# Scan parameters of an S5 block: their rows turned behind the third tile of x, and their element-wise work written for GpSimd

## The chip, the cores and the metric

The kernel runs on one core of a Trainium2 chip. The metric is the device time of one execution in microseconds; three runs of the kernel before gave a median of 1979.87 us (1978.76 to 1980.63). The core has a matrix engine (TensorE, PE in the profile; its weight loads are PEld), VectorE (DVE), ScalarE (ACT), GpSimd (POOL) and SyncE (SP), which only issues transfers here. Each engine works through its own list of instructions in order, and waits at an instruction until the results it needs are there.

## The reference

The input x is 1024 tokens by 1024 channels in fp32, and the network is two blocks. The first block:

```
h    = rmsnorm(x, norm_mix_pre)
proj = h @ w_in                       # q 512, k 128, v 128, u 512, two gates of 1024
attn = sliding_window_attention(q, k, v, sinks, rel_bias)     # 8 heads of 64, window 128
ssm  = s5_ssm(u, lam_re, lam_im, log_dt, b_re, b_im, c_re, c_im, d_skip)
x    = x + gated merge of attn and ssm @ w_out;  then a squared-ReLU MLP of width 4096
```

The second block is a gated hybrid layer with a last rmsnorm. The scan, s5_ssm, has 32 groups of 16 channels with 64 complex states each, and its parameters are made from a few small tensors:

```
dt = exp(log_dt);  mag = exp(lr * dt);  ab = mag * (cos(li * dt) + i sin(li * dt))
f  = (ab - 1) / (lr + i li);            bb = f * b;     h_t = ab * h_(t-1) + bb u_t;     y = Re(c h)
```

So there are 16 x 128 values each of lam_re (lr) and lam_im (li), an exponential and a sine and cosine of each, and powers of ab, before the scan can be written as matrix products.

## The kernel before

**Products.** Every fp32 operand of a product is split in two fp16 parts: ScalarE writes the high part (line 136), VectorE the low one (line 137, scalar_tensor_tensor, STT), and TensorE makes three fp16 products of each pair (lines 214 to 216). Most projections go by a seven-product scheme (the function strassen): VectorE adds halves of the weights and of the activations beforehand (lines 166 to 172) and joins partial results (u at lines 237 and 243, c at 259) afterwards. The first two projections (first_pair, line 399, PSUM tiles called pq) use the plain eight by three products, since these can start with the first columns of x.

**The start.** x comes in eight tiles of 128 tokens. For each, ScalarE sums the squares (line 581), VectorE forms mean plus epsilon (line 442, the [128,1] tile rs), GpSimd raises it to the power -0.5 (line 444, in place), VectorE scales the tile (line 582), TensorE turns it with eight transposes (line 464, PSUM tiles tr), and ScalarE and VectorE split what comes out. GpSimd does little else: the power of each norm, and the issue of small transfers. VectorE then makes the sums for the seven-product scheme (sums_later), TensorE goes on with k, v and the first half of q.

**The scan's parameters** (lines 648 to 791 of the kernel before) are a unit of their own, in the program behind the second half of q, strassen(w_in, 256, ...). lam_re, lam_im and log_dt are loaded as rows of 16 x 128 (L16, in a piece of SBUF at 142 KB called arena), turned by three small transposes on TensorE (plp, line 658), and copied to the tile prm (line 661). From there VectorE works on tiles of 128 partitions with 16 values each (128x16), 32 or 128: EXP for dt (lines 664 to 679: a range reduction and a polynomial, where ki is a conversion to integers), EXP for the magnitudes (128x32), seven multiples of the angle (line 728, 128x16 each), SINCOS (lines 681 to 717, 128x128), the first power of ab (lines 732 and 733), powers by squaring (cmul, lines 637 to 646), the factors f_r and f_i (lines 741 to 753), and Bf = f * b by cmul on 128x256. The raw b (braw) lies in the same piece of SBUF as L16, so its two transfers, which GpSimd issues at line 756, wait for the three transposes. Attention comes next in the program, then u, then the scan.

**Order.** The Tile framework takes the program's units and sets a fixed order for each engine when it is built; the instructions of one engine then stay in that order. A unit written earlier gets its instructions earlier on every engine.

Of the kernel before, what the change touches and what calls it, by code (L numbers as in the profile page):

```python
# [15 lines left out]
ALU = mybir.AluOpType  # L16

P = 128
# [16 lines left out]
LN2_HI = 0.693145751953125  # L35
LN2_LO = 1.42860682030941723e-6
PIO2_1 = 1.5703125
PIO2_2 = float(np.floor((np.pi / 2 - 1.5703125) * 2.0**22) / 2.0**22)
PIO2_3 = float(np.pi / 2 - 1.5703125 - PIO2_2)
# [12 lines left out]
def kernel(ctx: ExitStack, tc: tile.TileContext, I: dict, out: bass.AP):  # L52
    nc = tc.nc
# [13 lines left out]
    def A32(kb, n):  # L67
        o = int(kb * KB) // 4
        return arena[:, o:o + n]

    def A16(kb, n):
        o = int(kb * KB) // 2
        return arena16[:, o:o + n]
# [19 lines left out]
    def nm(s):  # L93
        uid[0] += 1
        return f"{s}_{uid[0]}"

    def q2(name, n=H):
        t = pw.tile([P, H], F32, tag="q2", name=nm(name), bufs=NQ)
        return t if n == H else t[:, 0:n]
# [4 lines left out]
    def aux(name):  # L104
        return pps.tile([P, H], F32, tag="aux", name=nm(name), bufs=4)
# [17 lines left out]
    def small(shape, tag, bufs=1, dt=F32):  # L123
        return psm.tile(list(shape), dt, tag=tag, name=nm(tag), bufs=bufs)

    TS, STT, TT = nc.vector.tensor_scalar, nc.vector.scalar_tensor_tensor, nc.vector.tensor_tensor
# [3 lines left out]
    ident = small([P, P], "ident")  # L130
# [12 lines left out]
    def load_k(W, rows, c0):  # L143

        raw = pw.tile([P, 4, 256], F32, tag="raw", name=nm("raw"), bufs=NR)
        nc.sync.dma_start(out=raw, in_=rows(W)[:, :, c0:c0 + 256])
        return raw
# [287 lines left out]
    def rstd(ss, n, eps, serial=False):  # L435

        v = small([P, 1], "rs_1") if serial else small([P, 1], "rs_v", 3)
        if ss.shape[1] == 2:
            TT(v, ss[:, 0:1], ss[:, 1:2], ALU.add)
            TS(v, v, 1.0 / n, eps, ALU.mult, ALU.add)  # L440
        else:
            TS(v, ss, 1.0 / n, eps, ALU.mult, ALU.add)
        r = v if serial else small([P, 1], "rs_r", 3)
        nc.gpsimd.tensor_tensor(r, v, mhalf, ALU.pow)  # L444
        return r
# [85 lines left out]
    def halves(a):  # L531
        return [a[:, 0:H], a[:, H:2 * H]]
# [14 lines left out]
    def bias_rows():  # L547

        relb = small([33, 8], "relb")
        nc.vector.memset(relb, 1.0)  # L550
        nc.gpsimd.dma_start(out=relb[0:32, :], in_=I["rel_bias"])
        hot, row = A32(88, 384)[0:33, :], A32(89.5, 384)[0:8, :]
        nc.gpsimd.dma_start(out=hot, in_=I["onehot"])
        pb = aux("pbias")
        MM(pb[0:8, 0:384], relb, hot, start=True, stop=True)
        nc.scalar.copy(row, pb[0:8, 0:384])
        nc.gpsimd.dma_start(out=sink, in_=I["sinks"][0].partition_broadcast(P))
# [6 lines left out]
        skew = bass.AP(bdr.tensor, bdr.offset + 127, [[8 * 384 - 1, P], [384, 8], [1, 256]])  # L564
        nc.sync.dma_start(out=bias_t, in_=skew)

    kv_raws = []

    @do
    def _():  # L570
        xin = [A32((72, 56)[t // 4] + 4 * (t % 4), D) for t in range(NT)]
        for t in range(NT):
            nc.sync.dma_start(out=xin[t], in_=x[t * P:(t + 1) * P, :])
            if t == 0:
                nc.sync.dma_start(out=g_pre, in_=I["norm_mix_pre"][0].partition_broadcast(P))
            if t == 1:
                kv_raws.extend(load_k(w_in, HALVES[h], 512) for h in range(2))
        for t in range(NT):
            h, junk = xin[t], A16(134, D).bitcast(BF16)
            ss = small([P, 1], "ss1", 3)  # L580
            ACT(junk, xin[t], AF.Square, accum_out=ss)
            STT(h, xin[t], rstd(ss, D, 1e-6, True), g_pre, ALU.mult, ALU.mult)
            put_T(halves(h), t, hC, a21_1, lambda q, t: K32[q][:, :, (t % 4) * P:(t % 4 + 1) * P], later=True)
            if t == 1:
                prepare(1)
                bias_rows()


    q_t = A32(56, 4 * T).rearrange("p (c t) -> p c t", c=4)
# [34 lines left out]
    dsk = A32(140, G * C)[0:C, :].rearrange("p (r a c) -> p r a c", r=NP, a=2)  # L624
# [4 lines left out]
    def tmp(n, kb=None):  # L629
        if kb is not None:  # L630
            return A32(kb, n)
        a = A32(toff[0], n)
        toff[0] += n * 4 / KB
        assert toff[0] <= 134
        return a
# [11 lines left out]

    @do
    def _():
        L16 = tmp(3 * P, 142)[0:16, :].rearrange("p (i m) -> p i m", i=3)  # L650
        nc.gpsimd.dma_start(out=L16[:, 0, :], in_=I["lam_re"][0].rearrange("(r a) p -> r (a p)", a=2))
        nc.gpsimd.dma_start(out=L16[:, 1, :], in_=I["lam_im"][0].rearrange("(r a) p -> r (a p)", a=2))
        ldt = small([16, 2], "ldt")
        nc.gpsimd.dma_start(out=ldt, in_=I["log_dt"][0].rearrange("(r a) -> r a", a=2))
        nc.vector.tensor_copy(L16[:, 2, :].rearrange("p (a q) -> p a q", a=2), ldt.unsqueeze(2).to_broadcast([16, 2, 64]))
        plp = aux("plp")
        for i in range(3):
            nc.tensor.transpose(plp[:, i * 16:(i + 1) * 16], L16[:, i, :], ident[0:16, 0:16])
        keep = q2("prm")
        prm = keep[:, 0:48].rearrange("p (i r) -> p i r", i=3)  # L660
        nc.vector.tensor_copy(prm, plp[:, 0:48].rearrange("p (i r) -> p i r", i=3))
        lr, li = prm[:, 0, :], prm[:, 1, :]

        def EXP(dst, src, n):
            save, toff[0] = toff[0], 131.0
            xc, t, k, r, p = (tmp(n) for _ in range(5))
            ki = tmp(n).bitcast(I32)
            TS(xc, src, -87.0, 88.0, ALU.max, ALU.min)
            TS(t, xc, LOG2E, MAGIC, ALU.mult, ALU.add)
            TS(k, t, -MAGIC, None, ALU.add)  # L670
            STT(r, k, -LN2_HI, xc, ALU.mult, ALU.add)
            STT(r, k, -LN2_LO, r, ALU.mult, ALU.add)
            TS(p, r, 1.0 / 5040, None, ALU.mult)
            for c in (1.0 / 720, 1.0 / 120, 1.0 / 24, 1.0 / 6, 0.5, 1.0):
                STT(p, p, c, r, ALU.add, ALU.mult)
            TS(p, p, 1.0, None, ALU.add)
            TS(ki, k, 127.0, 8388608.0, ALU.add, ALU.mult)
            TT(dst, p, ki.bitcast(F32), ALU.mult)
            toff[0] = save

        def SINCOS(sn, cs, y, n):
            save, toff[0] = toff[0], 131.0
            t, q, r, r2, p, c = (tmp(n) for _ in range(6))
            s, o = r, r2
            TS(t, y, 2.0 / np.pi, MAGIC, ALU.mult, ALU.add)
            TS(q, t, -MAGIC, None, ALU.add)
            STT(r, q, -PIO2_1, y, ALU.mult, ALU.add)
            STT(r, q, -PIO2_2, r, ALU.mult, ALU.add)
            STT(r, q, -PIO2_3, r, ALU.mult, ALU.add)
            TT(r2, r, r, ALU.mult)  # L690
            TS(p, r2, 1.0 / 362880, None, ALU.mult)
            for cc in (-1.0 / 5040, 1.0 / 120, -1.0 / 6):
                STT(p, p, cc, r2, ALU.add, ALU.mult)
            STT(s, p, 1.0, r, ALU.add, ALU.mult)
            TS(p, r2, -1.0 / 3628800, None, ALU.mult)
            for cc in (1.0 / 40320, -1.0 / 720, 1.0 / 24, -0.5):
                STT(p, p, cc, r2, ALU.add, ALU.mult)
            TS(c, p, 1.0, None, ALU.add)

            TS(t, q, 0.5, -0.25, ALU.mult, ALU.add)  # L700
            TS(t, t, MAGIC, None, ALU.add)
            TS(t, t, -MAGIC, None, ALU.add)
            STT(o, t, -2.0, q, ALU.mult, ALU.add)
            TS(p, t, 0.5, -0.25, ALU.mult, ALU.add)
            TS(p, p, MAGIC, None, ALU.add)
            TS(p, p, -MAGIC, None, ALU.add)
            STT(p, p, -2.0, t, ALU.mult, ALU.add)
            TS(p, p, -2.0, 1.0, ALU.mult, ALU.add)
            TT(t, c, s, ALU.subtract)
            TT(t, t, o, ALU.mult)  # L710
            TT(t, t, s, ALU.add)
            TT(sn, t, p, ALU.mult)
            TT(t, c, s, ALU.add)
            TT(t, t, o, ALU.mult)
            TT(t, c, t, ALU.subtract)
            TT(cs, t, p, ALU.mult)
            toff[0] = save
# [44 lines left out]
        for i, n_ in enumerate(("c_re", "c_im")):  # L762
# [7 lines left out]
                nc.vector.tensor_copy(CT[a * 64:(a + 1) * 64, i], v[:, :, a, :])  # L770

        nc.gpsimd.dma_start(out=dsk.rearrange("p r a c -> p (r a c)"), in_=I["d_skip"][0].partition_broadcast(C))
        TT(dsk.rearrange("p r a c -> p (r a) c"), dsk.rearrange("p r a c -> p (r a) c"),
           ident[0:C, 0:C].unsqueeze(1).to_broadcast([C, G, C]), ALU.mult)

        for i, cs in enumerate((csd, snd)):
# [1 line left out]
        for k in range(4):  # L778
            m = 1 << k
# [430 lines left out]
    class InFacc:  # L1210
        a = [A16(128, 4 * 4 * H).rearrange("p (t h k c) -> p h t k c", t=4, h=4, k=4)[:, i] for i in range(2)]
# [348 lines left out]
```

## Time and profile before

| | us |
|---|---|
| median of three runs | 1979.87 |
| the profiled execution | 1979.92 |
| its span, first to last instruction | 1978.2 |
| TensorE busy | 1920.3 (97%) |
| VectorE busy | 1530.9 (77%) |
| ScalarE busy | 898.9 (45%) |
| GpSimd busy | 91.6 (5%) |

The profiled execution stands 0.05 us from the median, and 1.7 us of it lie outside the span. Busy times add up the durations of an engine's instructions; engines work beside each other, so the shares don't add up to one. Where TensorE is busy nearly all the time, an edit moves the end only so far as it opens or closes gaps in TensorE's row.

### The profile page before, as it was taken

Reading aid. Unit: us, or ns where it says so; the run is one execution under the profiler, and the core shown is the slowest. Engines: PE = TensorE matmul, PEld = TensorE weight load, DVE = VectorE, ACT = ScalarE, POOL = GpSimd, SP = SyncE. Lnnn points to the kernel's source line nnn. Section 1 sums busy time; section 2 is a strip of 40 time slices with the busy share of each in tenths; the row PEclk is TensorE's granted clock in tenths of the full one; section 3 lists DMA queues with packets and bytes.
Section 4 is the critical chain, followed back from the end, with each engine's and each line's share of the span. In section 5 each row is a group of like instructions: output and inputs, shape, how many; then the busy total and the mean of one; then the engine's idle time right before and its main releaser. Section 6 shows DMA issues by size and latency. Waiting matters only on the chain. (4 is left out here: it accounts for less than half of the span.)

```text
span 1978.2 us, 25744 instructions
## 1 busy us (share of the span) xinstructions
PE 1920.3 (97%) x9462; PEld 909.8 (46%) x9462; DVE 1530.9 (77%) x2817; ACT 898.9 (45%) x1702; POOL 91.6 (5%) x155
## 2 busy tenths in 40 slices
PE   7989998999999999999999999999999999999998
PEld 4445444444444444444454444454444444444443
DVE  7897878969579858868867667689688897899843
ACT  8437543344347536526546545435343343444411
POOL 1000101100010000000000011000000000000000
PEclk9999999999999999999999999999999999999999
DMA  7211633787221211211223422111211233333122
GB/s 237 69 59 44 134 97 90 222 273 232 65 96 43 64 56 51 64 61 47 65 75 108 118 92 78 43 44 54 74 54 54 64 86 75 86 75 96 49 80 85
DMA packets 133727, 176.01 MB, mean 89 GB/s; under 512 B 12353, under 2 KB 99653, under 8 KB 133472
## 3 DMA queue, kind: packets, MB, share of 16 engines
q1 hardware_dynamic: 126000, 163.09, 26.0%
q0 software_dynamic: 5424, 10.22, 3.5%
q8 instruction: 74, 1.21, 0.3%
q10 hardware_dynamic: 2176, 1.05, 0.2%
q14 instruction: 53, 0.43, 0.1%
HBM read 139.58 MB, written 30.95 MB: 86 GB/s over the span
## 5 line engine op out<-in xcount | busy, mean ns | idle before, releaser
L214 PE MATMUL b<-arena,whi 128*128 128x512 f16 x2044 | 776.8, 380 | 11.1 <-DVE u L243 3.1
L215 PE MATMUL b<-arena,whi 128*128 128x512 f16 x2044 | 776.6, 380 | 0.9 <-DVE arena L137 0.9
L216 PE MATMUL b<-arena,wlo 128*128 128x512 f16 x2044 | 776.6, 380 | 0.0
L136 ACT ACTIVATE whi<-raw 128x512 f16<-128x512 f32 x553 | 332.2, 620 | 504.6 <-PE b L215 237.2
L137 DVE SCALAR_TENSOR_TENSOR wlo<-raw,whi 128x512 f16<-128x512 f32 x553 | 369.6, 678 | 73.6 <-ACT whi L136 72.3
L215 PEld LDWEIGHTS <-whi 128*128 128x128 f16 x2044 | 200.4, 98 | 253.4 <-issue 19.3
L216 PEld LDWEIGHTS <-wlo 128*128 128x128 f16 x2044 | 200.4, 98 | 242.2 <-issue 6.2
L214 PEld LDWEIGHTS <-whi 128*128 128x128 f16 x2044 | 200.4, 98 | 240.4 <-issue 5.0
L259 DVE SCALAR_TENSOR_TENSOR c<-b,u 128x512 f32<-128x512 f32 x204 | 139.4, 684 | 53.6 <-PE b L216 53.4
L431 PEld LDWEIGHTS <-arena 128*128 128x128 f16 x1152 | 112.7, 98 | 133.2
L368 PE MATMUL pl<-arena,whi 128*128 128x512 f16 x320 | 82.4, 379 | 1.7 <-DVE fetch L1023 1.7
L431 PE MATMUL po<-arena 128*128 128x512 f16 x384 | 84.0, 379 | 0.0
L431 PE MATMUL pf<-arena 128*128 128x512 f16 x384 | 84.0, 379 | 0.0
L431 PE MATMUL pw<-arena 128*128 128x512 f16 x384 | 83.0, 379 | 0.0
L399 PE MATMUL pq<-arena,whi 128*128 128x512 f16 (+1 forms) x288 | 79.8, 361 | 0.1
L237 DVE SCALAR_TENSOR_TENSOR u<-b,p 128x512 f32<-128x512 f32 x79 | 54.2, 686 | 29.7 <-PE b L216 27.6
L243 DVE SCALAR_TENSOR_TENSOR u<-b,u 128x512 f32<-128x512 f32 x79 | 54.2, 686 | 29.4 <-PE b L216 29.3
L865 ACT ACTIVATE c<-c 128x512 f32<-128x512 f32 x60 | 37.7, 628 | 63.1 <-DVE c L259 58.0
L450 ACT ACTIVATE hn<-xr 128x512 f32<-128x512 f32 x32 | 19.9, 622 | 90.5 <-issue 40.1
L232 ACT ACTIVATE p<-b 128x512 f32<-128x512 f32 x79 | 46.1, 584 | 29.3 <-PE b L216 29.2
L136 ACT ACTIVATE arena<-c 128x512 f16<-128x512 f32 x67 | 41.8, 625 | 29.0 <-DVE c L1398 20.8
L444 POOL TENSOR_TENSOR rs_r<-rs_v,mhalf 128x1 f32<-128x1 f32 x48 | 27.6, 575 | 530.5 <-DVE rs_v L440 452.5
(326 smaller groups left out, 2066.8 us busy)
## 6 DMA issues: line engine op xcount, KB each, us to landing
raw<-in_w_in_dram SPq DMA_DIRECT2D x86, 512.0 KB, 4.0
raw<-in_w_ff_in_dram SPq DMA_DIRECT2D x32, 512.0 KB, 4.0
raw<-in_w_ff_out_dram SPq DMA_DIRECT2D x32, 512.0 KB, 4.2
fetch<-gdr SPq DMA_DIRECT2D x32, 256.0 KB, 5.2
xr<-xdr SPq DMA_DIRECT2D x32, 256.0 KB, 3.5
gdr<-c SPq DMA_DIRECT2D x24, 256.0 KB, 2.1
arena<-in_x_dram SPq DMA_DIRECT2D x8, 512.0 KB, 9.9
raw<-in_w_out_dram SPq DMA_DIRECT2D x8, 512.0 KB, 6.5
```

What stands on the lines that cost most here:

```text
L136: ACT(hi, src, AF.Copy, scale=scale)
L137: STT(lo, src, scale, hi, ALU.mult, ALU.subtract)
L214: MM(b[:, 0:n], whi[:, k], act[0][:, i, k, sl], start=(first and k == 0), stop=False, skip_group_check=not first)
L215: MM(b[:, 0:n], whi[:, k], act[1][:, i, k, sl], start=False, stop=False, skip_group_check=not first)
L216: MM(b[:, 0:n], wlo[:, k], act[0][:, i, k, sl], start=False, stop=(k == nk - 1), skip_group_check=not first)
L232: ACT(v["p1"], o1, AF.Copy, scale=scale)
L237: STT(v["u2"], o2, scale, v["p1"], ALU.mult, ALU.add)
L243: STT(v["u3"], o, scale, v["u2"], ALU.mult, ALU.add)
L259: STT(d, vw(o), scale, vw(v[u]), ALU.mult, ALU.add)
L368: MM(bs[s], w[:, k], a[:, k, s * H:(s + 1) * H], start=(k == 0 and w is hi and a is act[0]), stop=(k == 3 and w is lo))
L399: MM(o, w[:, k % 4], a, start=(k == 0 and w is hi and a is ahi), stop=(k == 7 and w is lo))
L431: MM(bs[s], part(a), w[:, s * H:(s + 1) * H], start=(k == 0 and a is ahi and w is whi), stop=(k == nk - 1 and a is alo))
```

## The change

The three loads of the parameters' rows, the three transposes and the copy to prm leave the parameters' unit for a function of their own, scan_rows, which is called in the loop over the tiles of x behind tile 2. In the unit itself the local names TS and TT become GpSimd's tensor_scalar and tensor_tensor, and STT, which GpSimd does here in two steps, becomes a helper that issues a TS and a TT through a temporary. On VectorE stay the conversions to integers (ki), the reciprocal, the two memsets, cmul, and the copies.

```diff
--- before.py
+++ after.py
@@ -564,7 +564,21 @@
         skew = bass.AP(bdr.tensor, bdr.offset + 127, [[8 * 384 - 1, P], [384, 8], [1, 256]])
         nc.sync.dma_start(out=bias_t, in_=skew)
 
-    kv_raws = []
+    kv_raws, scan_in = [], []
+
+    def scan_rows():
+
+        L16 = A32(142, 3 * P)[0:16, :].rearrange("p (i m) -> p i m", i=3)
+        for i, n_ in enumerate(("lam_re", "lam_im")):
+            nc.gpsimd.dma_start(out=L16[:, i, :], in_=I[n_][0].rearrange("(r a) p -> r (a p)", a=2))
+        ldt = small([16, 2], "ldt")
+        nc.gpsimd.dma_start(out=ldt, in_=I["log_dt"][0].rearrange("(r a) -> r a", a=2))
+        nc.vector.tensor_copy(L16[:, 2, :].rearrange("p (a q) -> p a q", a=2), ldt.unsqueeze(2).to_broadcast([16, 2, 64]))
+        plp = aux("plp")
+        for i in range(3):
+            nc.tensor.transpose(plp[:, i * 16:(i + 1) * 16], L16[:, i, :], ident[0:16, 0:16])
+        scan_in.append(q2("prm"))
+        nc.vector.tensor_copy(scan_in[0][:, 0:48], plp[:, 0:48])
 
     @do
     def _():
@@ -584,6 +598,8 @@
             if t == 1:
                 prepare(1)
                 bias_rows()
+            if t == 2:
+                scan_rows()
 
 
     q_t = A32(56, 4 * T).rearrange("p (c t) -> p c t", c=4)
@@ -647,18 +663,16 @@
 
     @do
     def _():
-        L16 = tmp(3 * P, 142)[0:16, :].rearrange("p (i m) -> p i m", i=3)
-        nc.gpsimd.dma_start(out=L16[:, 0, :], in_=I["lam_re"][0].rearrange("(r a) p -> r (a p)", a=2))
-        nc.gpsimd.dma_start(out=L16[:, 1, :], in_=I["lam_im"][0].rearrange("(r a) p -> r (a p)", a=2))
-        ldt = small([16, 2], "ldt")
-        nc.gpsimd.dma_start(out=ldt, in_=I["log_dt"][0].rearrange("(r a) -> r a", a=2))
-        nc.vector.tensor_copy(L16[:, 2, :].rearrange("p (a q) -> p a q", a=2), ldt.unsqueeze(2).to_broadcast([16, 2, 64]))
-        plp = aux("plp")
-        for i in range(3):
-            nc.tensor.transpose(plp[:, i * 16:(i + 1) * 16], L16[:, i, :], ident[0:16, 0:16])
-        keep = q2("prm")
+
+        TS, TT = nc.gpsimd.tensor_scalar, nc.gpsimd.tensor_tensor
+
+        def STT(out, in0, c, in1, op0, op1, t=None):
+            t = in0 if t is None else t
+            TS(t, in0, c, None, op0)
+            TT(out, t, in1, op1)
+
+        keep = scan_in[0]
         prm = keep[:, 0:48].rearrange("p (i r) -> p i r", i=3)
-        nc.vector.tensor_copy(prm, plp[:, 0:48].rearrange("p (i r) -> p i r", i=3))
         lr, li = prm[:, 0, :], prm[:, 1, :]
 
         def EXP(dst, src, n):
@@ -668,13 +682,13 @@
             TS(xc, src, -87.0, 88.0, ALU.max, ALU.min)
             TS(t, xc, LOG2E, MAGIC, ALU.mult, ALU.add)
             TS(k, t, -MAGIC, None, ALU.add)
-            STT(r, k, -LN2_HI, xc, ALU.mult, ALU.add)
-            STT(r, k, -LN2_LO, r, ALU.mult, ALU.add)
+            STT(r, k, -LN2_HI, xc, ALU.mult, ALU.add, t)
+            STT(r, k, -LN2_LO, r, ALU.mult, ALU.add, t)
             TS(p, r, 1.0 / 5040, None, ALU.mult)
             for c in (1.0 / 720, 1.0 / 120, 1.0 / 24, 1.0 / 6, 0.5, 1.0):
                 STT(p, p, c, r, ALU.add, ALU.mult)
             TS(p, p, 1.0, None, ALU.add)
-            TS(ki, k, 127.0, 8388608.0, ALU.add, ALU.mult)
+            nc.vector.tensor_scalar(ki, k, 127.0, 8388608.0, ALU.add, ALU.mult)
             TT(dst, p, ki.bitcast(F32), ALU.mult)
             toff[0] = save
 
@@ -684,9 +698,9 @@
             s, o = r, r2
             TS(t, y, 2.0 / np.pi, MAGIC, ALU.mult, ALU.add)
             TS(q, t, -MAGIC, None, ALU.add)
-            STT(r, q, -PIO2_1, y, ALU.mult, ALU.add)
-            STT(r, q, -PIO2_2, r, ALU.mult, ALU.add)
-            STT(r, q, -PIO2_3, r, ALU.mult, ALU.add)
+            STT(r, q, -PIO2_1, y, ALU.mult, ALU.add, t)
+            STT(r, q, -PIO2_2, r, ALU.mult, ALU.add, t)
+            STT(r, q, -PIO2_3, r, ALU.mult, ALU.add, t)
             TT(r2, r, r, ALU.mult)
             TS(p, r2, 1.0 / 362880, None, ALU.mult)
             for cc in (-1.0 / 5040, 1.0 / 120, -1.0 / 6):
@@ -700,7 +714,7 @@
             TS(t, q, 0.5, -0.25, ALU.mult, ALU.add)
             TS(t, t, MAGIC, None, ALU.add)
             TS(t, t, -MAGIC, None, ALU.add)
-            STT(o, t, -2.0, q, ALU.mult, ALU.add)
+            STT(o, t, -2.0, q, ALU.mult, ALU.add, p)
             TS(p, t, 0.5, -0.25, ALU.mult, ALU.add)
             TS(p, p, MAGIC, None, ALU.add)
             TS(p, p, -MAGIC, None, ALU.add)
@@ -770,7 +784,7 @@
                 nc.vector.tensor_copy(CT[a * 64:(a + 1) * 64, i], v[:, :, a, :])
 
         nc.gpsimd.dma_start(out=dsk.rearrange("p r a c -> p (r a c)"), in_=I["d_skip"][0].partition_broadcast(C))
-        TT(dsk.rearrange("p r a c -> p (r a) c"), dsk.rearrange("p r a c -> p (r a) c"),
+        nc.vector.tensor_tensor(dsk.rearrange("p r a c -> p (r a) c"), dsk.rearrange("p r a c -> p (r a) c"),
            ident[0:C, 0:C].unsqueeze(1).to_broadcast([C, G, C]), ALU.mult)
 
         for i, cs in enumerate((csd, snd)):
```

The two orders, engine by engine. First GpSimd's list from the pow of tile 3 of x on, before (arena is SBUF scratch, rs_34 the rs tile of tile 3, then 4, 5, 6 and 7; in_b_re_dram is the raw b):

```order
L444 TENSOR_TENSOR rs_34_194<-rs_34_194,mhalf_75 128x1
L444 TENSOR_TENSOR rs_38_216<-rs_38_216,mhalf_75 128x1
L444 TENSOR_TENSOR rs_42_238<-rs_42_238,mhalf_75 128x1
L444 TENSOR_TENSOR rs_46_260<-rs_46_260,mhalf_75 128x1
L444 TENSOR_TENSOR rs_50_282<-rs_50_282,mhalf_75 128x1
L756 DMA arena<-in_b_re_dram 128x16x16
L756 DMA arena<-in_b_im_dram 128x16x16
```

and from the same place after the change (rs_37 is tile 3, rs_41 tile 4; lines 671 to 684 are EXP, 756 to 758 the denominator of f):

```order
L444 TENSOR_TENSOR rs_37_205<-rs_37_205,mhalf_75 128x1
L770 DMA arena<-in_b_re_dram 128x16x16
L770 DMA arena<-in_b_im_dram 128x16x16
L682 TENSOR_SCALAR arena<-prm_201 128x16
L756 TENSOR_TENSOR prm_201<-prm_201 128x16
L757 TENSOR_TENSOR prm_201<-prm_201 128x16
L444 TENSOR_TENSOR rs_41_227<-rs_41_227,mhalf_75 128x1
L683 TENSOR_SCALAR arena<-arena 128x16
L758 TENSOR_TENSOR prm_201<-prm_201 128x16
L684 TENSOR_SCALAR arena<-arena 128x16
L671 TENSOR_SCALAR arena<-arena 128x16
L672 TENSOR_TENSOR arena<-arena 128x16
```

The two transfers of b now stand between the pows of tiles 3 and 4, with three element-wise instructions; 21 more stand between tiles 4 and 5, 31 between 5 and 6, nine (two on 128x32, seven on 128x128) between 6 and 7, and 44 behind tile 7. GpSimd's whole list grows from 143 rows to 252.

VectorE's list where it reads tiles 5 and 6 of x, before (rs_42 is tile 5, rs_46 tile 6; lines 442 and 582 are the mean and the scaling):

```order
L442 TENSOR_SCALAR rs_42_238<-ss_41_236 128x1
L582 SCALAR_TENSOR_TENSOR arena<-arena,rs_42_238 128x1024
L442 TENSOR_SCALAR rs_46_260<-ss_45_258 128x1
L137 SCALAR_TENSOR_TENSOR arena<-tr_220,arena 128x4x128
L137 SCALAR_TENSOR_TENSOR arena<-tr_225,arena 128x4x128
L582 SCALAR_TENSOR_TENSOR arena<-arena,rs_46_260 128x1024
```

and after (rs_45 is tile 5, rs_49 tile 6; line 596 is the scaling, 691 the conversion ki, 759 the reciprocal):

```order
L442 TENSOR_SCALAR rs_45_249<-ss_44_247 128x1
L691 TENSOR_SCALAR arena<-arena 128x16
L759 RECIPROCAL prm_201<-prm_201 128x16
L596 SCALAR_TENSOR_TENSOR arena<-arena,rs_45_249 128x1024
L691 TENSOR_SCALAR arena<-arena 128x32
L137 SCALAR_TENSOR_TENSOR arena<-tr_231,arena 128x4x128
L137 SCALAR_TENSOR_TENSOR arena<-tr_236,arena 128x4x128
L442 TENSOR_SCALAR rs_49_271<-ss_48_269 128x1
L596 SCALAR_TENSOR_TENSOR arena<-arena,rs_49_271 128x1024
```

Three instructions that read what GpSimd makes now stand between VectorE's work on the tiles of x. VectorE's list shrinks from 2722 rows to 2646; the block of cmul begins at its row 72, and u2 and u3 of the first seven-product projection stand at rows 119 and 129, where they stood at 78 and 80. On TensorE the three transposes plp stand behind six pq products that follow tile 2's transposes; the first logits of attention come 120 products of lines 214 to 216 earlier than before.

## Rows read from the trace of the kernel before

**Rows 1.** The page's head: span, and busy us of each engine.
```profile
span 1978.2 us, 25744 instructions
...
PE 1920.3 (97%) x9462; PEld 909.8 (46%) x9462; DVE 1530.9 (77%) x2817; ACT 898.9 (45%) x1702; POOL 91.6 (5%) x155
```

**Rows 2.** Windows: stretch, us, busy by engine (instructions), TensorE's clock, DMA, GB/s.
```profile
20.00:40.00 20.00, 19.38 (x149) 15.86 (x148) 16.40 (x27) 18.47 (x37) 2.74 (x5) 1.00 0.75 222
...
100.00:140.00 40.00, 33.74 (x147) 16.34 (x146) 37.20 (x166) 11.73 (x37) 1.50 (x2) 0.91 0.18 60
...
130.00:140.00 10.00, 7.35 (x23) 3.92 (x22) 8.78 (x39) 6.89 (x29) 0.00 (x0) 0.66 0.14 54
40.00:60.00 20.00, 20.00 (x94) 9.06 (x93) 20.00 (x18) 13.86 (x18) 0.00 (x0) 1.00 0.14 41
```

**Rows 3.** TensorE's waits, 100 to 140 us: total, times, longest.
```profile
PE b L214 <- DVE u L237: 1.8, 1, 1.8
...
PE b L214 <- DVE arena L706: 0.8, 1, 0.8
```

**Rows 4.** Timeline of GpSimd (POOL): start, us, instruction, idle before and releaser.
```profile
32.15 0.55 POOL L444 TENSOR_TENSOR rs<-rs,mhalf 128x1 f32<-128x1 f32 x1 [2.52 <-DVE rs L442]
...
88.81 1.23 POOL L756 DMA_DIRECT2D arena<-in_b_re_dram  x1 [56.12 <-PE plp L658]
93.62 1.18 POOL L756 DMA_DIRECT2D arena<-in_b_im_dram  x1 [3.58 <-issue]
```

**Rows 5.** Timeline of TensorE (PE), the same columns.
```profile
20.75 0.42 PE L399 MATMUL pq<-arena,whi 128*128 128x256 f16 x1
20.96 0.42 PE L399 MATMUL pq<-arena,wlo 128*128 128x256 f16 x1
...
35.30 1.26 PE L464 MATMUL tr<-ident,arena 128*128 128x128 f32 x8 [0.55 <-ACT arena L499]
...
70.00 0.38 PE L214 MATMUL b<-arena,whi 128*128 128x512 f16 x1
...
88.22 0.35 PE L658 MATMUL plp<-ident,arena 16*128 16x16 f32 x3
```

**Rows 6.** Timeline of VectorE (DVE) at tile 7 of x.
```profile
31.85 0.15 DVE L442 TENSOR_SCALAR rs<-ss 128x1 f32<-128x1 f32 x1 [0.53 <-ACT arena L136]
32.73 1.28 DVE L582 SCALAR_TENSOR_TENSOR arena<-arena,rs 128x1024 f32<-128x1024 f32 x1 [0.73 <-POOL rs L444]
```

**Rows 7.** Timeline of GpSimd, its first element-wise instructions.
```profile
0.31 0.10 POOL L1546 MEMSET const-float32-0.0<- 128x1 f32 x1 [0.31 <-issue]
...
2.26 0.33 POOL masks.py:199 TENSOR_SCALAR_AFFINE_SELECT ident<-ident 128x128 f32<-128x128 f32 x1
```

**Rows 8.** Timeline of GpSimd, tile 0's pow.
```profile
11.08 0.88 POOL L444 TENSOR_TENSOR rs<-rs,mhalf 128x1 f32<-128x1 f32 x1 [1.80 <-DVE rs L442]
```

**Rows 9.** Timeline of VectorE beside GpSimd's work.
```profile
10.84 1.50 DVE L137 SCALAR_TENSOR_TENSOR wlo<-raw,whi 128x512 f16<-128x512 f32 x2
...
93.96 0.17 DVE L726 TENSOR_TENSOR prm<-prm,dt 128x16 f32<-128x16 f32 x1
94.08 0.69 DVE L723 TENSOR_SCALAR prm<-prm 128x16 f32<-128x16 f32 x1
```

**Rows 10.** Groups of VectorE by shape, 88 to 140 us: busy, mean ns.
```profile
L697 DVE SCALAR_TENSOR_TENSOR arena<-arena 128x128 f32<-128x128 f32 x4 | 1.2, 289 | 0.1
...
L675 DVE SCALAR_TENSOR_TENSOR arena<-arena 128x16 f32<-128x16 f32 x6 | 1.0, 174 | 0.2
...
L639 DVE TENSOR_TENSOR arena<-prm,arena 128x256 f32<-128x256 f32 x1 | 0.4, 417 | 0.0
```

**Rows 11.** Timeline of VectorE at the first seven-product projection.
```profile
63.42 0.69 DVE L166 TENSOR_TENSOR raw<-raw,raw 128x512 f32<-128x512 f32 x1
...
75.45 0.69 DVE L237 SCALAR_TENSOR_TENSOR u<-b,p 128x512 f32<-128x512 f32 x1 [1.52 <-PE b L216]
...
77.97 0.69 DVE L243 SCALAR_TENSOR_TENSOR u<-b,u 128x512 f32<-128x512 f32 x1 [1.23 <-PE b L216]
```

## The prediction

> **What bounds the kernel now.** I read the page's head first: TensorE is busy 1920.3 of 1978.2 us [rows 1], so an edit moves the end only through the 57.9 us in which TensorE has nothing to do. Next the windows [rows 2]. From 20 to 40 us, where this change puts work, TensorE is busy 19.38 of 20 us: a delay there is a delay of the end, unless something later gives it back. From 100 to 140 us it is busy 33.74 of 40, so 6.26 us are idle, and its granted clock is 0.91 on the mean, down to 0.66 in the last ten microseconds (between the two levels, 1.2 and 2.4 GHz, some of both). VectorE is busy 37.20 of these 40 us, and the waits name it: 1.8 us for u, 0.8 us for a step of SINCOS [rows 3]. So there VectorE sets the pace, with the scan's parameters among its work, and that is what can be won.
>
> **Where the new work stands.** GpSimd now raises one number per row to a power for each tile of x, in 0.55 us [rows 4]; from this comes VectorE's scaling, then the turn on TensorE, in a list that is in order. After the change the two transfers of b and 64 element-wise instructions stand in GpSimd's list ahead of the pow of tile 7, and tiles 4 to 7 each wait for a part of them. TensorE's list has no other work to put there: the transposes of tiles 4 to 7 stand between the pq products, in order.
>
> First the time at which GpSimd can begin. The transfers of b wait for the transposes plp, which stand six pq products behind tile 2's. These products begin at 20.75 us, 0.21 us apart, and three small transposes take 0.35 us [rows 5]: 20.75 + 6 x 0.21 + 0.35 = 22.4, with the hand-over 22.55. In the trace of before the two issues run from 88.81 to 94.80, 5.99 us, of which 3.58 us are a gap ahead of the second that no other engine explains [rows 4]. That gives 28.5 us. If the gap doesn't recur, 2.41 us are left and it is 25.0; with DMA at 0.75 [rows 2] it can also be longer than in a quieter stretch, and I allow 3 us more. I take 28.5.
>
> Then the price of one dependent instruction on GpSimd, which the trace doesn't show for 16 elements. The hand-over: tile 7's mean ends at 32.00 on VectorE and its pow starts at 32.15 [rows 4, 6], so 0.15 us. Its own time is at least that of the smallest memset, 0.10 us, and a pow of one element takes 0.55 [rows 4, 7]. So p lies between 0.10 (no hand-over within the engine) and 0.55 us; I take 0.15 + 0.12 = 0.27, since a multiplication is nearer to the memset than a power is. For 128 columns the nearest row is the select on 128x128, 0.33 us [rows 7]; with the hand-over w = 0.48, bounds 0.2 and 0.8.
>
> Ahead of tile 7's pow: 50 dependent small instructions x 0.27 = 13.5; the seven independent multiples of the angle x 0.10 = 0.7; seven wide ones x 0.48 = 3.4; the pows of tiles 4 to 7, 4 x 0.55 = 2.2; VectorE's two conversions in between, there and back, 0.5. Sum 20.3, so tile 7's pow ends at 28.5 + 20.3 = 48.8 us. Before, it ended at 32.70 [rows 4]: 16.1 us later. Of this 1.3 us is slack: tile 7 was scaled at 34.01 [rows 6] and its transposes began at 35.30, waiting for ScalarE at the last [rows 5]. **The start loses 14.8 us**, bounds 0.8 (p 0.10, w 0.2, no gap: 34.8 us) and 31 (p 0.55, w 0.8: 65.0 us). VectorE's and ScalarE's work on the tiles shifts along with it.
>
> Two smaller terms. While TensorE waits from tile to tile its clock may fall, as in the stretch of 130 to 140 us, where idle time and a clock of 0.66 stand together and 3.4 us of clock are lost [rows 2]; between 0 and 3.4 I take 1. And GpSimd and VectorE slow each other: a pow took 0.88 us instead of 0.55 beside two low-part splits of VectorE [rows 8, 9], and a VectorE instruction on 16 columns 0.69 instead of 0.17 beside the issue of b_im [rows 4, 9]. Before tile 7 VectorE mostly waits itself; for the rest I take 2, bounds 0 and 14 (below).
>
> **What is removed and moved.** VectorE loses 34 instructions on 128 columns x 0.29 and some 44 small ones x 0.17 [rows 10], about 17 us, and the cmul that stays on it moves ahead of the stretch of 100 to 140 us. The idle time of that stretch, 6.26 us, and its clock, 40 x 0.09 = 3.6, are the most that can come back: 9.9 us. Not all of it will, since the wait for c_re's transfer and attention's own waits for VectorE stay. I take 6.5, bounds 0 and 9.9. Behind VectorE there, the next limit is TensorE itself. The order brings attention 120 products forward (26 us at 0.21); that moves work, and takes none away.
>
> Three edits I cost at nothing. The 44 instructions behind tile 7, 44 x 0.48 = 21, end near 70 us; VectorE reaches the cmul that needs them where line 166 began at 63.42 [rows 11], now at 78.2: 8 us of cover. The 44 rows of cmul ahead of u3, some 10 us at 0.17 to 0.42 [rows 10], fit in about: VectorE's old work in that stretch, 10.3 us, and these end at 63.4 + 20 = 83 by the old times, and TensorE, which makes a product group in 2.5 us [rows 11], needs u3 gone at 70.0 + 5 x 2.59 = 83 [rows 5]. With VectorE late, this cover is the first to go. And the copy and the three transposes cost the same at either place.
>
> **The sum.** 1979.92 + 14.8 + 1 + 2 - 6.5 = 1991 us. The profiled execution stands at the median of the runs (0.05 us off), so this is also the forecast for the median. Its own range, with p from 0.18 to 0.40 (tile 7's pow 4.5 us sooner or 6.5 later), is 1985 to 2000.
>
> **Rivals.**
> (B) GpSimd's small instructions are cheap, and the loss at the start falls under the gain. With p 0.10, w 0.33 and no gap before b_im, tile 7's pow ends at 25.0 + 5.0 + 0.7 + 2.3 + 2.2 + 0.5 = 35.7, the start loses 1.7, and with 6.5 to 9.9 back the time is 1972 to 1975, say 1974: faster. With the gap it loses 5.2, and 1979 is no change. It decides from a loss under 2.5 us on. For it: memsets of 0.10 us follow one another without a wait. Against it: the pow's 0.55 us for one element, a hand-over of 0.15 wherever an instruction waits for another, and the 3.58 us gap [rows 4, 6].
> The Trainium skill speaks for a price near B's: "GPSIMD Engine Reference", section 3.1, gives an add of two fp32 inputs with 2048 columns as 4497 ns at about 2.6 cycles per element. An estimate from that page is about 0.1 us for 16 columns and 0.34 for 128, without waits, and the sum by it would be B's with the gap. No row here shows GpSimd adding or multiplying, and its one-element pow of 0.55 us is well above that estimate.
> (C) The two engines shut each other out behind tile 7. From 40 to 60 us VectorE is busy 20.0 of 20 [rows 2], with work on SBUF; if each of the 44 instructions adds 0.33 us as the pow did [rows 8], GpSimd ends 14.5 us later, at 84, VectorE waits for it at the cmul or has lost as much itself, u2 and u3 come late, and TensorE waits up to that time: 1991 + 13 = 2004. For it: the two slowed instructions above; against it: one of them stood beside the issue of a transfer, not beside arithmetic.
> The Trainium skill states this as a rule: by "SBUF — State Buffer", section "SBUF: two separate sides", GpSimd and a VectorE instruction with two SBUF inputs take a shared port pair by turns, each for the whole instruction. The pow at 0.88 us agrees with that [rows 8, 9]; whether it also holds up VectorE on the path, no row shows.
> (D) GpSimd's arithmetic costs as much as its pow, p = 0.55: the start loses 31 us, and GpSimd ends at 65 + 44 x 0.8 = 100 where VectorE wants it at 94: 1979.9 + 31 + 1 + 2 - 6.5 + 3 = 2010.
> That the framework would hide the change doesn't arise: the order of each list is known.
>
> **How the numbers follow.** Forecast 0.45, B 0.25, C 0.15, D 0.15. This kernel's runs tell about 0.2%, 4 us, from no change, so faster is below 1976 and slower above 1984. Slower: 0.40 of the forecast's 0.45 (a cheap p with the full gain falls short of it), C and D, 0.70. No change: 0.05 of the forecast and 0.07 of B, 0.12. Faster: the rest of B, 0.18. The range reaches from the lower part of B to D, 1974 to 2010; what is left out are B with the full gain, and D with both engines in each other's way.
>
> **What would show it.** Right: the pows of tiles 4 to 7 at about 29, 36, 45 and 48 us, each behind an instruction of GpSimd's; tile 7's transposes near 50 us instead of 35.3; idle time of TensorE between 20 and 50 us named after VectorE's scaling, and VectorE's after GpSimd; no wait at the cmul; less than 2 us idle where 100 to 140 us stood before. Wrong in the first step: the second transfer of b issued at 24 us, or dependent instructions less than 0.2 us apart. Wrong in the cover: GpSimd's last product of SINCOS later than VectorE's line 166, and TensorE waiting for u. Wrong in the gain: the same idle time beside attention although VectorE has room.

## The result and the profile after

Slower: the median of four runs is 2001.12 us (1999.58 to 2003.55), beside 1980.11 for the kernel before; the ratio is 1.0107, 95% interval 1.0095 to 1.0119, so 21 us. The profiled execution took 2000.92 us with a span of 1999.2, which is 21.0 us more than in [rows 1]. (The row in [rows 8] is tile 1's pow, not tile 0's as its line says; nothing hangs on that. And GpSimd has 115 new element-wise instructions, 270 beside 155: 64 stand ahead of tile 7's pow, as was counted, and 51 behind it; the 44 of the count are those up to the product that cmul waits for.)

The page's head after the change, busy us by engine:

```profile
span 1999.2 us, 25776 instructions
...
PE 1925.1 (96%) x9462; PEld 913.1 (46%) x9462; DVE 1523.6 (76%) x2731; ACT 898.1 (45%) x1702; POOL 151.8 (8%) x270
```

TensorE's work is the same 9462 matmuls. Of the 21.0 us, 16.2 are time in which it has nothing to do (74.1 us beside 57.9) and 4.8 are longer busy time, for which the windows below show a lower clock. GpSimd's busy time went from 91.6 to 151.8 us, and VectorE's fell by only 7. The place of the loss is in the windows (stretch, us, busy by engine, TensorE's clock, DMA, GB/s):

```profile
20.00:40.00 20.00, 12.13 (x73) 9.40 (x72) 6.82 (x14) 9.30 (x18) 12.38 (x33) 0.87 0.78 222
40.00:60.00 20.00, 12.69 (x72) 10.00 (x71) 8.47 (x14) 7.56 (x15) 16.96 (x46) 0.70 0.00 0
...
100.00:120.00 20.00, 12.44 (x38) 4.74 (x38) 18.60 (x64) 7.34 (x15) 0.00 (x0) 0.75 0.18 52
```

From 20 to 60 us, where TensorE had 0.62 us idle [rows 2], it now has 15.2, and the clock is down as well; a second hole of 7.6 us stands at 100 to 120. TensorE's timeline in the start shows who waits, by the transposes of tiles 4 to 7 of x:

```profile
31.29 1.67 PE L464 MATMUL tr<-ident,arena 128*128 128x128 f32 x8 [3.79 <-DVE arena L596]
39.73 1.94 PE L464 MATMUL tr<-ident,arena 128*128 128x128 f32 x8 [4.08 <-DVE arena L596]
51.14 1.94 PE L464 MATMUL tr<-ident,arena 128*128 128x128 f32 x8 [6.05 <-DVE arena L596]
57.21 1.07 PE L464 MATMUL tr<-ident,arena 128*128 128x128 f32 x8 [1.26 <-DVE arena L596]
```

Tile 7's begin at 57.21 instead of 35.30 [rows 5]: 21.9 us late, which is the whole of the change's 21.0, since 0.9 came back behind them. VectorE's scaling, which they wait for, itself waits for GpSimd's pows. GpSimd's timeline there (start, us, instruction):

```profile
22.82 1.22 POOL L770 DMA_DIRECT2D arena<-in_b_re_dram  x1 [2.03 <-PE plp L579]
27.28 1.17 POOL L770 DMA_DIRECT2D arena<-in_b_im_dram  x1 [3.24 <-PE tr L464]
...
29.91 1.29 POOL L683 TENSOR_SCALAR arena<-arena 128x16 f32<-128x16 f32 x1
...
31.93 0.27 POOL L671 TENSOR_SCALAR arena<-arena 128x16 f32<-128x16 f32 x1
32.29 0.27 POOL L672 TENSOR_TENSOR arena<-arena 128x16 f32<-128x16 f32 x1
32.65 0.25 POOL L671 TENSOR_SCALAR arena<-arena 128x16 f32<-128x16 f32 x1
...
40.28 1.73 POOL L742 TENSOR_SCALAR prm<-prm 128x16 f32<-128x16 f32 x7
...
54.98 0.58 POOL L444 TENSOR_TENSOR rs<-rs,mhalf 128x1 f32<-128x1 f32 x1
55.53 0.45 POOL L672 TENSOR_TENSOR arena<-arena 128x128 f32<-128x128 f32 x1
...
62.62 2.45 POOL L671 TENSOR_SCALAR arena<-arena 128x128 f32<-128x128 f32 x1
...
94.49 0.22 POOL L746 TENSOR_TENSOR arena<-mags,arena 128x16 f32<-128x16 f32 x1
```

Read the starts, not the durations: a dependent small instruction takes 0.22 to 0.27 us and the next one starts 0.31 to 0.36 after it. The pow of tile 7 stands behind that chain, at 54.98, and the last product that cmul waits for ends at 94.71. Two instructions stick out, 1.29 us on 16 columns and 2.45 on 128, where the same kinds take about 0.2 and 0.53 elsewhere. VectorE's timeline at these places:

```profile
29.86 1.29 DVE L596 SCALAR_TENSOR_TENSOR arena<-arena,rs 128x1024 f32<-128x1024 f32 x1 [6.37 <-POOL rs L444]
31.06 1.28 DVE L137 SCALAR_TENSOR_TENSOR arena<-tr,arena 128x512 f16<-128x512 f32 x2
...
62.14 2.54 DVE L522 TENSOR_TENSOR arena<-arena 128x2048 f32<-128x2048 f32 x1
...
94.74 0.17 DVE L654 TENSOR_TENSOR arena<-arena 128x16 f32<-128x16 f32 x1 [6.09 <-POOL arena L746]
```

The scaling from 29.86 to 31.15 has two sources in SBUF, and GpSimd's 1.29 us end with it, at 31.20; the split behind it reads PSUM and SBUF, and the instructions beside it run at their usual pace. The last row is the cover that was counted on: the first product of cmul waits 6.09 us for GpSimd.

### The profile page after: what moved, and what is told of

It reads as the page before. It is cut to its first block, busy times and chain, and to the rows that moved or that the text cites. A ratio compares the mean times of both kernels' runs of the same rounds, so it can differ in the third digit from the quotient of the medians.

```text
span 1999.2 us, 25776 instructions
## 1 busy us (share of the span) xinstructions
PE 1925.1 (96%) x9462; PEld 913.1 (46%) x9462; DVE 1523.6 (76%) x2731; ACT 898.1 (45%) x1702; POOL 151.8 (8%) x270
## 5 line engine op out<-in xcount | busy, mean ns | idle before, releaser
L399 PE MATMUL pq<-arena,whi 128*128 128x512 f16 (+1 forms) x288 | 84.0, 375 | 0.0
L232 ACT ACTIVATE p<-b 128x512 f32<-128x512 f32 x79 | 46.1, 583 | 29.6 <-PE b L216 29.5
```

Source lines behind the costliest of these rows:

```text
L232: ACT(v["p1"], o1, AF.Copy, scale=scale)
L399: MM(o, w[:, k % 4], a, start=(k == 0 and w is hi and a is ahi), stop=(k == 7 and w is lo))
```

## The experiments

Three theories. Q: the chain on GpSimd, in order ahead of the pows, delays tiles 4 to 7 and through them TensorE. R: turning the rows early, with the early transfers of b, is what costs. P: GpSimd and VectorE shut each other out, behind tile 7 above all. All kernels start from the changed one; times are compared with the kernel before on the same chip. Where an expectation counts 102 instructions on GpSimd, or 55 behind tile 7's pow, the kernels have 115 and 68.

**Rows early, arithmetic on VectorE.**
```diff
-        TS, TT = nc.gpsimd.tensor_scalar, nc.gpsimd.tensor_tensor
...
+            nc.vector.scalar_tensor_tensor(out, in0, c, in1, op0, op1)
```


> The rows are turned behind tile 2 as in the change, but all the arithmetic of the parameters stays on VectorE. Theory Q (the pows of tiles 4 to 7 stand behind GpSimd's chain of element-wise instructions): the chain is gone, only the two transfers of b (5.6 us) remain ahead of tile 4's pow; tile 7's transposes at about 41 us (35.3 before, 57.2 with the change), time 1980 to 1986. Theory R (turning the rows early and fetching b there is what costs): tile 7's transposes at 50 us or later, time 1995 or more. Theory P (GpSimd and VectorE shut each other out): like Q, with VectorE's instructions at their durations of before.

1980.11 us beside 1979.58, ratio 1.0005 (0.9996 to 1.0014): no change, as Q has it. Tile 7's transposes in its timeline:

```profile
41.20 1.04 PE L464 MATMUL tr<-ident,arena 128*128 128x128 f32 x8
```

5.9 us late, by the transfers of b ahead of tile 4's pow; and that came back later, where the parameters are now ready before attention: from 80 to 140 us TensorE is idle for 4.3 us instead of 6.3, at a mean clock of 0.97 instead of 0.94. R falls: with the rows alone the change costs nothing, so GpSimd's arithmetic is what costs.

**GpSimd's arithmetic, rows at their old place.**
```diff
-            if t == 2:
-                scan_rows()
...
+        scan_rows()
         keep = scan_in[0]
```


> The arithmetic goes to GpSimd as in the change, but the rows are turned where they were before, behind the second half of q. Theory Q: no instruction of the scan stands ahead of a pow, tile 7's transposes at 35.3 as before; GpSimd's 102 instructions begin near 95 us and take 35 us at 0.34 each, 89 us at the 0.87 that they took behind tile 7; VectorE's cmul, which now comes before much of its other work, waits for them. If that wait holds up what TensorE needs, 1990 to 2030, else 1974 to 1980. Theory R: as fast as before or faster, 1974 to 1980. Theory P: GpSimd's instructions between 100 and 140 us take as long as VectorE's that stand beside them with two SBUF sources, up to 0.7 us and more each.

2010.95, ratio 1.016 (1.0143 to 1.0178), within Q's 1990 to 2030; R falls here too. The start is as before (transposes at 35.45), and the end is worse than with the change: GpSimd's arithmetic runs from 95.1 to 146.2, cmul waits for the chain, and the raw c, whose transfer stands behind the chain in GpSimd's queue, comes late. VectorE's and TensorE's largest waits (for what: us, times, longest):

```profile
DVE arena L790 <- POOL arena L725: 25.7, 1, 25.7
```
```profile
PE pc L780 <- DMA arena<-in_c_re_dram: 28.5, 1, 28.5
```

VectorE stands waiting beside the sines here, so GpSimd's chain can be seen alone. The first and the last of the 44 instructions that stand behind tile 7's pow in the changed kernel:

```profile
120.49 0.45 POOL L670 TENSOR_TENSOR arena<-arena 128x128 f32<-128x128 f32 x1
...
142.77 0.22 POOL L745 TENSOR_TENSOR arena<-mags,arena 128x16 f32<-128x16 f32 x1
```

That is 22.5 us, where the changed kernel took 39.2 for the same 44 (55.53 to 94.71) beside a busy VectorE.

**The whole change, rows behind tile 7.**
```diff
-            if t == 2:
+            if t == 7:
```


> The whole change, with the rows turned behind tile 7 instead of tile 2, so that all pows come first. Theory Q alone (only the order ahead of the pows costs): tile 7's transposes at 35.3, GpSimd's 102 instructions from 45 us on at 0.34 to 0.6 each, done by 90, no stall to speak of: 1974 to 1981. Theory P (each GpSimd instruction waits out a VectorE instruction with two SBUF sources, and VectorE is full here): 0.87 us each, done near 130 us; VectorE waits at cmul from about 78 us on, u2 stands behind it, TensorE stops for 30 us or more: 2000 to 2030. Theory R: between these, start as before.

2008.07, ratio 1.0142 (1.0118 to 1.0167), as P has it. Start undisturbed (35.88), then TensorE waits 29.6 us for u, behind VectorE, which waits 26.0 for GpSimd:

```profile
PE b L214 <- DVE u L243: 29.6, 1, 29.6
```

GpSimd is done at 110.6 and not near 130 as P has it, since from 78.9 on, while VectorE waits, its steps run undisturbed. Here the two engines can be laid side by side, GpSimd first, then VectorE:

```profile
44.25 2.15 POOL L683 TENSOR_SCALAR arena<-arena 128x16 f32<-128x16 f32 x1
46.48 0.54 POOL L758 TENSOR_TENSOR prm<-prm 128x16 f32<-128x16 f32 x1
47.10 2.19 POOL L684 TENSOR_SCALAR arena<-arena 128x16 f32<-128x16 f32 x1
```
```profile
44.06 2.28 DVE L523 TENSOR_TENSOR arena<-arena 128x2048 f32<-128x2048 f32 x1
46.26 0.68 DVE L166 TENSOR_TENSOR raw<-raw,raw 128x512 f32<-128x512 f32 x1
46.86 2.30 DVE L524 TENSOR_TENSOR arena<-arena 128x2048 f32<-128x2048 f32 x1
```

Each of these instructions of GpSimd on 16 columns, 0.2 to 0.3 us elsewhere, ends with VectorE's: 46.40 and 46.34, 47.02 and 46.94, 49.29 and 49.16. VectorE's own keep their durations (2.28 and 2.30). The Trainium skill, "SBUF — State Buffer", section "SBUF: two separate sides", has this as a lock on a shared port pair for a VectorE instruction with two SBUF inputs, held for the whole instruction; these rows agree, with GpSimd as the one that pays.

**b on SyncE.**
```diff
-            nc.gpsimd.dma_start(out=braw[:, i], ...)
+            nc.sync.dma_start(out=braw[:, i], ...)
```


> The whole change, but the two transfers of b are issued by SyncE instead of GpSimd. Theory Q: 5.6 us less stand ahead of tile 4's pow; tile 7's transposes at about 51.7 instead of 57.2, time 1995 to 1996. Theory R (the early transfer of b is most of the cost): 1985 or less. Theory P: GpSimd still ends some 38 us behind tile 7's pow, and TensorE still waits for u and its splits near 100 us.

1996.86, ratio 1.0092 (1.0073 to 1.011). Tile 7's transposes:

```profile
52.19 1.07 PE L464 MATMUL tr<-ident,arena 128*128 128x128 f32 x8 [0.93 <-DVE arena L596]
```

They come 5.0 us sooner than with the change, and the loss against the kernel before is 17.3 us instead of 21.0, so 3.7 less. Both are Q's, within a microsecond. P's part came too: TensorE still waits 3.6 us for u and 4.0 for its splits, so Q and P don't exclude each other here.

**Exponentials on VectorE, the rest on GpSimd**, b on SyncE.
```diff
         def EXP(dst, src, n):
+            TS, TT = nc.vector.tensor_scalar, nc.vector.tensor_tensor
...
```


> The whole change with b on SyncE, but the two exponentials stay on VectorE; GpSimd keeps the multiples of the angle, the sines and the factors, 55 instructions behind tile 7's pow. Theory Q: three instructions stand ahead of the pows, so the start loses 1 to 2 us instead of 16.9. Theory P: each of the 34 wide steps (47 instructions) costs 0.6 us alone and up to 2.5 beside a VectorE instruction with two SBUF sources; GpSimd ends 33 to 45 us after it begins, and VectorE's cmul, with u behind it, waits: time 1980 to 1995. If GpSimd's work is free once no pow stands behind it: 1972 to 1976.

1997.53, ratio 1.0089 (1.0073 to 1.0105), 2.5 us beyond P's range. The start is clean (36.15) and 18 us go all the same: GpSimd's work begins at 71.5, when VectorE has the first exponential ready behind its sums, and ends at 106.9; for 19.7 of these 35.4 us VectorE waits and nobody is in the way, and a wide step starts 0.55 to 0.61 us after the one before:

```profile
88.03 0.53 POOL L671 TENSOR_SCALAR arena<-arena 128x128 f32<-128x128 f32 x1
88.64 0.46 POOL L672 TENSOR_TENSOR arena<-arena 128x128 f32<-128x128 f32 x1
89.19 0.53 POOL L711 TENSOR_SCALAR arena<-arena 128x128 f32<-128x128 f32 x1
```

VectorE's wait for that chain, behind which TensorE waits 15.7 us:

```profile
DVE arena L793 <- POOL arena L728: 19.7, 1, 19.7
```

So P is not only the lock: a chain of 47 wide steps is long by itself.

**Exponentials on GpSimd, the rest on VectorE**, b on SyncE (the mirror of the last).
```diff
         def SINCOS(sn, cs, y, n):
-            TS(t, y, 2.0 / np.pi, MAGIC, ALU.mult, ALU.add)
+            nc.vector.tensor_scalar(t, y, 2.0 / np.pi, MAGIC, ALU.mult, ALU.add)
...
```


> The other half of the split: the two exponentials and their scalars on GpSimd (46 instructions, among the pows of tiles 3 to 7), the multiples, the sines and the factors on VectorE, b on SyncE. Theory Q: the 46 instructions ahead of tile 7's pow at the 0.33 us that they took in the changed kernel are 15 us, less the 1.3 of slack: tile 7's transposes at 46 to 49 instead of 35.3; nothing of GpSimd's is left for cmul to wait for, so the start's loss of 11 to 14 us, less 4 to 6 us that the earlier rows give back, is the whole: 1985 to 1990. Theory P: the time is lost behind tile 7, so this half is free: 1976 to 1982.

1996.45, ratio 1.0087 (1.0074 to 1.0101), 6 us above what Q expected. The transposes begin at 49.88, a microsecond beyond its range, 14.6 late; but nothing was given back. TensorE waits 2.6 us for the copy of c ahead of the logits, and then runs at half the clock for 20 us, which no expectation had; its busy time is 10.4 us longer than in the kernel before (windows):

```profile
110.00:115.00 5.00, 4.31 (x12) 1.96 (x12) 2.85 (x18) 0.00 (x0) 0.00 (x0) 0.54 0.66 198
115.00:120.00 5.00, 5.00 (x14) 2.31 (x14) 3.38 (x20) 1.16 (x5) 0.00 (x0) 0.50 0.00 0
```

Either half of the arithmetic costs 17 to 18 us, and both together (the run with b on SyncE) 17. Where the start is late, VectorE comes to cmul later and waits 6.1 us for GpSimd instead of the 19.7 of the clean start, so most of the second wait is covered by the first. The exponentials' 17 hold the stretch at half the clock, so that they equal the others is in part chance.

**Rows early, arithmetic on VectorE as in the first experiment, b on SyncE.**
```diff
...
-            nc.gpsimd.dma_start(out=braw[:, i], ...)
+            nc.sync.dma_start(out=braw[:, i], ...)
```


> Rows turned behind tile 2, all arithmetic on VectorE, and b fetched by SyncE, so GpSimd has only its pows. With the rows alone the start lost 5.9 us (tile 7's transposes at 41.2 instead of 35.3) and the time was that of before, so 5.9 us came back later. If the two transfers of b ahead of tile 4's pow are all of that loss (theory Q), the transposes are at 36 and the time is 1974 to 1976. If the loss comes from VectorE's small instructions between the tiles, they stay at 40 to 41 and the time at 1980.

1979.34 beside 1979.60, ratio 0.9999 (0.9991 to 1.0008). The transposes are at 36.10, as expected; the time isn't. A wait for c doesn't explain it: TensorE waits 3.6 us for its transfer here, and 3.5 for VectorE's copy with the rows alone. In the two traces the lead is still 4.1 us at the last products of attention (tile pvo, 190.00 against 194.06), but the profiled execution here, 1976.73, is the shortest of eleven, so where the median loses the rest isn't shown.

**Rows behind tile 7, arithmetic on VectorE as in the first experiment.**
```diff
-            if t == 2:
+            if t == 7:
...
```


> Rows turned behind tile 7, all arithmetic on VectorE, b still issued by GpSimd, now behind all pows. Theory Q: no pow waits, tile 7's transposes at 35.3 to 35.9 as in the whole change with the rows behind tile 7, and what the earlier rows give back stays: 1974 to 1977. If VectorE, full from 40 to 60 us, is the limit there, the parameters' work delays the sums behind it and u comes late: 1979 to 1983.

1977.06 beside 1979.60, ratio 0.9989 (0.9981 to 0.9998): 2 us faster, at the edge of what can be told. TensorE waits 3.5 us for VectorE and 2.2 for the second transfer of c.

**The raw c in a free piece of SBUF**, with the rows behind tile 2 and then behind tile 7.
```diff
...
-            craw = tmp(256, 133).rearrange("p (u q) -> p u q", u=4)
+            craw = tmp(256, 144 + i).rearrange("p (u q) -> p u q", u=4)
```


> As the kernel with rows behind tile 2, VectorE's arithmetic and b on SyncE, and in addition the raw c lies in a free piece of SBUF (144 and 145 KB) instead of one that cmul uses, so its transfers wait for nothing of VectorE's. With the rows alone TensorE waited 3.5 us for the copy of c behind VectorE; if that wait is on the path: 3 to 4 us less than the kernel without this edit, 1970 to 1973; if VectorE is late with the rest of attention's inputs anyway, the same time as without.

> Rows behind tile 7, all arithmetic on VectorE, and the raw c in a free piece of SBUF. In the kernel without the second edit TensorE waited 5.7 us for the two turns of c behind VectorE and the transfer. If these waits go and attention is not late in turn: 1972 to 1975. If the wait only moves to the logits, as with the rows behind tile 2 (3.4 us there, and 20 us at a granted clock of 0.5 behind it): 1978 to 1986.

The first: 1984.54, ratio 1.0027 (1.0013 to 1.004), 5 us slower. The wait for c is gone and stands 3.41 us long at the logits, and behind it TensorE is busy at half its clock (windows of the two runs, the first and the second):

```profile
95.00:100.00 5.00, 4.55 (x11) 1.92 (x12) 3.52 (x14) 0.24 (x1) 0.00 (x0) 0.51 0.00 0
100.00:105.00 5.00, 5.00 (x12) 1.67 (x11) 2.04 (x14) 0.36 (x1) 0.00 (x0) 0.50 0.00 0
```
```profile
80.00:100.00 20.00, 16.84 (x76) 7.64 (x74) 17.82 (x78) 3.38 (x6) 0.00 (x0) 0.91 0.00 0
100.00:120.00 20.00, 20.00 (x91) 9.34 (x91) 18.33 (x91) 9.08 (x37) 0.00 (x0) 1.00 0.00 1
```

The second: 1974.27 beside 1979.21, ratio 0.9976 (0.996 to 0.9992), 5 us faster than the kernel before and the best of all. Its six times reach from 1971.17 to 1980.33, and the profiled execution, 1978.36, lies in the upper part, so its trace doesn't show what the shortest ones had. Its wait at the logits is 3.2 us too, but the clock comes back within that stretch. Why it does in the one and not in the other stays open: the waits are of a length.

## Why the prediction was right, step by step

The way was right: the change is slower, and by the path that was forecast, from GpSimd's chain through the pows and VectorE's scaling to TensorE. The sum was too low. 2001 us lies 10 above the forecast and 1 above its own range of 1985 to 2000; only the wide range, which also takes in C and D, holds it. Two parts erred the same way: the start's loss by 7.1 us, and the three small terms, 0.9 us won where 3.5 were forecast, by 2.6.

- **GpSimd's beginning.** Forecast 28.5 us; b_im's issue ended at 28.45. The gap ahead of it recurred, 3.24 us instead of 3.58 [rows 4].
- **The price of a small instruction** was too low: p = 0.27, and the 20 of the second exponential take 7.0 us, 0.35 each (+4 over 50). The multiples of the angle cost 0.25 each and not 0.10 (+1.1), a wide step 0.57 and not 0.48 (+0.6). The Trainium skill's figures ("GPSIMD Engine Reference", section 3.1), from which 0.1 us was estimated for 16 columns, are further off: 0.22 to 0.27 for the instruction alone. The measurement decides.
- **The lock ahead of tile 7** wasn't in the sum. VectorE "mostly waits itself" there, but its scaling doesn't, and three instructions stood behind one (1.29, 1.13 and 1.13 us instead of 0.2 to 0.3): +2.8. Together 8.5; the span shows 6.7 more, since independent instructions start only 0.17 us apart and GpSimd never waited for VectorE's two conversions, counted at 0.5.
- **The start's loss**, 14.8 forecast, is 21.9: GpSimd needed 27.0 us for what was counted as 20.3, and the transposes are 7.1 later than forecast. This is the term that was mis-sized. With GpSimd's arithmetic the loss goes to the end about one for one: 21.9 and 21.0; 16.9 and 17.3 with b on SyncE; 14.6 and 17.2 with the exponentials alone, where the half clock takes a part. With VectorE's arithmetic 5.9 us came back.
- **The cover at cmul** failed: GpSimd ended at 94.7, not 70. It began 6.8 us later than forecast, and the 44 instructions took 0.89 us each, 39.2 in all instead of 21. Alone they take 22.5, as the run with the rows at their old place shows, so the price of a wide step was about right, and working beside VectorE added 16.7, where C has 14.5. That is rival C on top of the forecast, with 6.1 us of waiting on VectorE and two waits of 3.9 on TensorE instead of C's 13: the late start and VectorE's own slower sums had moved VectorE to 88.6 by then.
- **The gain** of 6.5 us can't be seen apart from the failed cover. TensorE's idle time from 100 to 140 us was 6.3 [rows 2] and is 7.7, now nearly all of it the two waits of the cover. VectorE's busy time fell by 7.3 us and not by 17; 2.9 of the difference are its sums beside the sines, the rest isn't traced.
- **The rivals.** B (cheap instructions) fell with the prices, and D (as dear as the pow) with 0.35 against 0.55. C's time, 2004, is nearer to 2001 than the forecast's 1991, and its mechanism is there. But it is made of 14.8 at the start and 13 at the cover, and measured are 21.9 and 7.8, so that its number fits so well is luck.

## What to carry to other kernels

A free engine's queue isn't free when the path has one instruction in it: ask what stands behind the new work in that queue, and count dependent steps at the spacing of their starts, not at their durations. A chain of steps on 16 columns costs more than half of what one on 128 does (0.35 us against 0.57 from start to start); it belongs on the engine whose single step is shortest, or where nobody waits for its end. And where one wait covers another, taking away one of them wins little: either half of the arithmetic alone cost as much as both. So an edit is tried alone and with the next wait taken away too.

## What the runs showed of the hardware

GpSimd, beside a VectorE instruction with two sources in SBUF, stretches to that instruction's end (0.2 to 2.2 us), while VectorE's keeps its 2.28 us when GpSimd's are 16 columns wide. With 128 columns VectorE pays as well: its sums from line 522 to 528 took 24.4 us beside the sines (62.14 to 86.57), 21.5 in the kernel before (40.07 to 61.58). Ahead of its second issue for b, GpSimd stands idle for 2.7 to 4.0 us in seven of the kernels, wherever the issue stands (3.58 in the kernel before, 3.24 with the change, 2.73 with the rows behind tile 7); what it waits for isn't shown. TensorE's granted clock after waits of 2.6 and 3.4 us near 100 us was 0.50 (1.2 GHz) for some 20 us in two kernels (exponentials on GpSimd; rows behind tile 2 with c apart); after 3.2 us in the kernel with rows behind tile 7 and c apart it was 0.91 over 80 to 100 and 1.00 behind.
